# A decoder layer in fp32: state updates as row tiles, fp32r transposes, a column-tiled gate product, and another order of units

## The chip, the cores and the metric

The program runs on one core of a Trainium2 chip. The metric is the time of one execution on the device in microseconds, the median of several runs. Everything works in fp32: weights and activations come from memory as fp32, and the large products run on TensorE in a form called fp32r, of which three products make up one fp32 product.

## The reference

One layer handles a prompt of 256 tokens and 8 samples of 8 new tokens each, 320 columns in all, which share every weight. `c` conditions the layer through `w_ada`; the sample tokens start from a stored attention state and stored pooling rows.

```python
mod = jax.nn.silu(c) @ w_ada + b_ada
sh1, sc1, g1, sh2, sc2, g2 = split(mod, 6)                 # each 2048 wide
h = rmsnorm(x, norm1_g) * (1 + sc1) + sh1
q, k, v, og, u, ga, gb, alr = split(h @ w_in)              # 1024 1024 2048 2048 1024 2048 2048 16
loga = log_sigmoid(alr @ w_a2 + b_a) / 16
# per head (4 heads, 256 x 512), in chunks:  S = diag(exp(b_last)) S + kd^T v;  o = qe S + (causal qe ke^T) v
o, s_new = _gla(q, k, v, loga, s0)
y_a = rmsnorm(o, gla_norm_g) * silu(og)
d = (mean of the last 2, 4, 8 or 16 rows of u, by head) - u
y_b = (d @ w_pool[head]) * pool_scale
x = x + g1 * ((sigmoid(ga) * y_a + sigmoid(gb) * y_b) @ w_o)
h2 = rmsnorm(x, norm2_g) * (1 + sc2) + sh2
x = x + g2 * ((silu(gate) * up) @ w_down)                  # gate, up = split(h2 @ w_gu), 5632 each
y = rmsnorm(x, final_norm_g)
```

The outputs are y for the prompt and the samples, the new attention state of both and the new pooling rows of both.

## The kernel before

Activations stand transposed: 128 channels on the partitions, 320 tokens along the row, 16 such tiles for 2048 channels. Each fp32 matrix is used as a sum of two fp32r parts, hi and lo. ScalarE (ACT) casts a weight chunk to its hi part (L157), VectorE (DVE) subtracts to get the lo part (L158), and `mm3` makes three products (L171 to L173: hi by hi, hi by the activation's lo part, lo by hi).

`proj` takes one unit of 256 output columns: 16 channel tiles, two halves, three products, so 96 products of 320 columns with weights of 128 x 128 into one PSUM tile. Raw weights come on the SyncE queue. Such a unit's PSUM tile comes from the pool `pmain`, which has two; all small products take one-bank tiles from `pmisc`, which has four, through `misc()`.

**Stages.** In the head stage the rows of x are normed, the first sections of the modulation are made, and the units of attention head 0 are computed in six slices of the channels (`SLICES`); in its last slice stands `alr_proj`, the gate rank product. Then come heads 1 to 3, eleven units each, in the order q, k, v, v, u, og, og, ga, ga, gb, gb. After that w_o with x1 (8 units), the second norm, the FFN in two parts (44 units of gate and up, 8 units of w_down, each part), and the final norm with transposes of x into rows (L1107 and the lines around it).

**What sets the order.** Attention and pooling of a head are lists of steps (`gla_steps`, `pool_steps`). They stand in a queue, and `pump` takes up to ten of them after each unit. So the steps of head 0 lie between the units of head 1, and those of head 1 partly between those of head 2. The steps of a head join the queue after its unit u. `s_y`, the pooling product with w_pool (PSUM tiles `psy`, taken from `pmain`), stands for head 0 in the middle of the steps, after the attention's exponentials:

```python
    queue += pst + st[:PSY] + [sig0] + psy + st[PSY:] + [merge_step(g0, E)]
    RATE = 10
    BURST_UNITS = (None, (1, 3, 9, 10)) + ((0, 1, 2, 3, 6, 8, 9, 10),) * 2
    LOAD_UNITS = (None, (0, 1, 7, 9, 10)) + ((0, 1, 2, 5, 6, 8, 9, 10),) * 2
```

The rest of the modulation is made in bursts of column-tiled fp32 products (`ada_burst`, L301), placed by `BURST_UNITS`; their weights `araw` are loaded on the GpSimd (POOL) queue (L269) at the places in `LOAD_UNITS`. Within this, a scheduler that simulates the engines moves instructions among each other, unless `high_priority` or `issue_after` binds them.

**The steps that matter here.** All are per head. `s_att` makes the causal products within 32-row blocks as column tiles (L682, 32 records), and the cross products (L687). `s_nat2` and `s_kpn` transpose v and k of the samples with `tr` (L135, an fp32 product with the identity). `s_kpn` copies each sample's 32 rows of k into its own quarter of a zeroed tile `kpn` (named w in the order), so that a product over all 128 rows updates one sample's state. `s_state` does two such updates: a product into a `misc()` tile (L807), then state times decay plus product on DVE (L809). `s_load` loads four samples' states `S`, two tiles of 1 MB at a time (two buffers), and the store `o_gs` empties them. `s_inter` (L782, L786) multiplies queries by the states as column tiles. `s_gk` multiplies `alr`, the gate rank rows, by `w_a2` (L591).

The last lines compute the norm of y: squares summed in `acc2` by DVE, three products with ones, then Sqrt and reciprocal for each of three row blocks, and six scalings (L1121 on ACT), each with its store.

Of the kernel before, what the change touches and what calls it, by code (L numbers as in the profile page):

```python
# [11 lines left out]
F32 = mybir.dt.float32  # L12
# [8 lines left out]
P = 128  # L21
# [3 lines left out]
D = 2048  # L25
# [54 lines left out]
def body(tc, A):  # L80
# [55 lines left out]


    more = []
    last_raw = []
    last_mm = []  # L140
# [11 lines left out]
    def split(raw):  # L152
# [5 lines left out]
        V.tensor_sub(lo, raw, hi.bitcast(F32))  # L158
        return hi, lo
# [15 lines left out]
    def proj(w, col, k0, k1, xh, xl, between=None):  # L175

        ps = pmain.tile([P, 2, 512], F32, tag="pm", name=nm("ps"))
        for c0 in range(k0, k1, 4):
            nk = min(4, k1 - c0)
            for j, whi, wlo in split_chunk(w[:, c0:c0 + nk, col:col + 256], nk, 256):  # L180
                kt = c0 + j
                for i in range(2):
                    mm3(ps[:, i, :T], whi[:, i * P:(i + 1) * P], wlo[:, i * P:(i + 1) * P],
                        xh[kt], xl[kt], kt == k0, kt == k1 - 1)
            if between:
                between(c0 - k0)
# [167 lines left out]
    def new_group(h):  # L354
# [5 lines left out]
        g.u = gp.tile([P, 2, UEW], F32, tag="u", name=nm("u"))  # L360
        return g

    def new_gates(g):
        g.og = gp.tile([P, 4, T], F32, tag="og", name=nm("og"))
        g.ga = merged[2] if g.h == 0 else None
        g.gb = merged[g.h]
# [36 lines left out]
    def gates(g, kind, i, src):  # L403
        og, gb = g.og[:, 2 * i:2 * i + 2, :], g.gb[:, 2 * i:2 * i + 2, :]
        if kind == "gb":
            S.activation(gb, src, AF.Sigmoid)
            return
        sg = gp.tile([P, 2, T], F32, tag="sg", name=nm("sg"))
# [12 lines left out]


    with tc.tile_pool(name="head", bufs=1) as xp:
# [8 lines left out]
        make_identity(nc, ident)  # L432
        pt = misc()
# [57 lines left out]
        def alr_proj(walr, cum):  # L491
            V.tensor_copy(cumr, cum)
            pa = misc()
            for k0 in range(0, KT, 8):
                wal = []
                for tag in ("whi", "wlo"):
                    t = wp.tile([P, 8, 64], F32R, tag=tag, bufs=WB, name=nm("wal"))
                    G.memset(t.bitcast(F32), 0.0)
                    wal.append(t)
                wk = walr[:, k0:k0 + 8]  # L500
                S.copy(wal[0][:, :, 0:16], wk)
                V.tensor_sub(wal[1][:, :, 0:16], wk, wal[0][:, :, 0:16].bitcast(F32))
# [4 lines left out]
            G.memset(alr[32:33, :], 1.0)  # L507
            V.tensor_copy(alr[0:16, 0:T], pa[0:16, 0:T])
# [637 lines left out]
```

## Time and profile before

| | |
|---|---|
| three runs | 1977.17, 1979.94, 1980.54 us |
| median | 1979.94 us |
| the profiled execution | 1972.99 us |
| its span (first to last instruction) | 1971.2 us |
| mean granted TensorE clock | 0.993 |
| memory read, written | 373.90 MB, 24.67 MB |

The profile comes from one execution. Its rows read as follows. A group of instructions has its line, engine and operation, then out<-in by the program's names, the shape (partitions x elements), its count, busy time and the mean ns of one, and at the end the idle time of that engine just before them with what ended it. PE is TensorE's matmul, PEld its weight load, which overlaps PE. Matmul records overlap each other too: one of 320 columns lasts about 310 ns, while the next starts sooner, so what a product costs is read from start to start. The chain that ended last lists, in order of time, the work that each step waited for, with start and length. The stages view gives, for each stretch, its length, the busy time and count of PE, PEld, DVE, ACT and POOL, the granted clock (1.00 is full speed), the busy share of the DMA engines and GB/s.

### The profile page before, as it was taken

To read this page: it belongs to the slowest core of one execution; us is meant where nothing else is said; L and a number is where in the kernel's file an instruction comes from. 1 tells how busy PE (TensorE), PEld (TensorE's weight loads), DVE (VectorE), ACT (ScalarE), POOL (GpSimd) and SP (SyncE) were. 2 spreads that over 40 slices of the span, in tenths; PEclk is the share of its full clock that TensorE was granted. 3 is DMA by queue.
4 is the path that set the end of the run, shared out by engine and by line. 5 is a ranking of instruction groups with operands and counts; after the bars stand their busy time and mean duration, and the time that the engine had idled before them with its cause. 6 is when DMAs were issued, how large, how long until landed. Compare 5 with 4: busy or idle time off the path is not lost.

```text
span 1971.2 us, 34613 instructions
## 1 busy us (share of the span) xinstructions
PE 1924.5 (98%) x13808; PEld 1825.2 (93%) x13808; DVE 1007.0 (51%) x1935; ACT 826.9 (42%) x1485; POOL 207.3 (11%) x323
## 2 busy tenths in 40 slices
PE   5999999999999999999999999999999999999997
PEld 4889888988998899989989999999999999999997
DVE  3776454666355535665574444444444444444554
ACT  4433343544345433553354333333333434344443
POOL 2231131221121112111030000000000000000000
PEclk9999989999999999999999999999999999999998
DMA  9996647777875788579845555444545444444442
GB/s 349 354 354 237 203 150 264 219 230 251 256 223 188 247 268 272 183 249 321 269 153 158 186 188 182 145 150 144 156 145 155 150 150 150 150 151 144 149 139 98
DMA packets 287308, 400.60 MB, mean 203 GB/s; under 512 B 11953, under 2 KB 243921, under 8 KB 286809
## 3 DMA queue, kind: packets, MB, share of 16 engines
q1 hardware_dynamic: 250170, 261.81, 42.7%
q0 software_dynamic: 36976, 136.57, 19.5%
q8 instruction: 108, 1.77, 0.4%
q14 instruction: 54, 0.44, 0.1%
HBM read 373.90 MB, written 24.67 MB: 202 GB/s over the span
## 4 chain that ended last, share of the span: by engine, by line
PE 82%; DMA 3%; ACT 1%; DVE 0%; issue 0%; POOL 0%; ACTq 0%; DVEq 0%
PE ps L172 25%; PE ps L171 25%; PE ps L173 25%; PE pm L301 3%; PE pm L135 1%; DMA araw<-w_ada 1%; PE pm L786 1%; PE pm L807 1%; DMA raw<-w_o 1%; DMA S<-state_gla 1%; PE pm L752 1%; DMA o_gs<-S 0%; PE pm L782 0%; PE pm L591 0%; PE pm L741 0%; PE psy L171 0%
## 5 line engine op out<-in xcount | busy, mean ns | idle before, releaser
L158 DVE TENSOR_TENSOR wlo<-raw,whi 128x512 fp32r<-128x512 f32 x952 | 657.7, 694 | 792.4 <-ACT whi L157 779.9
L157 ACT CAST whi<-raw 128x512 fp32r<-128x512 f32 x952 | 587.8, 622 | 948.3 <-PE ps L172 830.1
L171 PE MATMUL ps<-hh,whi 128*128 128x320 f32 x1408 | 441.9, 314 | 6.1 <-ACT hh L337 2.6
L172 PE MATMUL ps<-hl,whi 128*128 128x320 f32 x1408 | 440.4, 313 | 0.0
L173 PE MATMUL ps<-hh,wlo 128*128 128x320 f32 x1408 | 437.4, 312 | 0.0
L172 PE MATMUL ps<-h2l,whi 128*128 128x320 f32 x1408 | 434.7, 309 | 0.0
L171 PE MATMUL ps<-h2h,whi 128*128 128x320 f32 x1408 | 434.7, 309 | 0.0
L173 PE MATMUL ps<-h2h,wlo 128*128 128x320 f32 x1408 | 434.2, 309 | 0.0
L171 PEld LDWEIGHTS ps<-hh,whi 128*128 128x128 f32 x1408 | 265.2, 188 | 19.7 <-issue 9.0
L172 PEld LDWEIGHTS ps<-hl,whi 128*128 128x128 f32 x1408 | 265.3, 188 | 10.4 <-issue 9.4
L173 PEld LDWEIGHTS ps<-hh,wlo 128*128 128x128 f32 x1408 | 264.7, 188 | 8.0 <-issue 5.3
L171 PEld LDWEIGHTS ps<-h2h,whi 128*128 128x128 f32 x1408 | 264.4, 188 | 3.4 <-ACT ah L337 3.4
L172 PEld LDWEIGHTS ps<-h2l,whi 128*128 128x128 f32 x1408 | 264.5, 188 | 0.1
L173 PEld LDWEIGHTS ps<-h2h,wlo 128*128 128x128 f32 x1408 | 264.5, 188 | 0.0
L171 PE MATMUL ps<-ah,whi 128*128 128x320 f32 x704 | 217.7, 309 | 0.0
L172 PE MATMUL ps<-al,whi 128*128 128x320 f32 x704 | 216.5, 308 | 0.0
L173 PE MATMUL ps<-ah,wlo 128*128 128x320 f32 x704 | 216.5, 308 | 0.0
L172 PEld LDWEIGHTS ps<-al,whi 128*128 128x128 f32 x704 | 132.0, 187 | 0.0
L171 PEld LDWEIGHTS ps<-ah,whi 128*128 128x128 f32 x704 | 131.9, 187 | 0.0
L173 PEld LDWEIGHTS ps<-ah,wlo 128*128 128x128 f32 x704 | 131.9, 187 | 0.0
L269 POOL DMA_DIRECT2D araw<-w_ada x64 | 55.1, 864 | 397.2 <-PE pm L301 385.9
L172 PE MATMUL ps<-ml,whi 128*128 128x320 f32 x256 | 79.3, 310 | 0.0
(282 smaller groups left out, 1634.2 us busy)
## 6 DMA issues: line engine op xcount, KB each, us to landing
raw<-w_gu SPq DMA_DIRECT2D x176, 512.0 KB, 3.5
raw<-w_in SPq DMA_DIRECT2D x170, 512.0 KB, 4.4
araw<-w_ada POOLq DMA_DIRECT2D x64, 1024.0 KB, 8.7
raw<-w_down SPq DMA_DIRECT2D x80, 512.0 KB, 3.5
hraw<-w_ada POOLq DMA_DIRECT2D x28, 1024.0 KB, 9.8
S<-state_gla POOLq DMA_DIRECT2D x16, 1024.0 KB, 8.3
o_gs<-S POOLq DMA_DIRECT2D x16, 1024.0 KB, 6.9
raw<-w_o SPq DMA_DIRECT2D x32, 512.0 KB, 6.2
```

The source lines that it names most:

```text
L135: PE.transpose(out, in_, ident[:k, :k])
L157: S.copy(hi, raw)
L158: V.tensor_sub(lo, raw, hi.bitcast(F32))
L171: PE.matmul(ps, lhsT=whi, rhs=xhi, start=start, stop=False)
L172: PE.matmul(ps, lhsT=whi, rhs=xlo, start=False, stop=False)
L173: last_mm[:] = [PE.matmul(ps, lhsT=wlo, rhs=xhi, start=False, stop=stop).ins]
L269: nc.gpsimd.dma_start(t[:, r:r + step], wada[:, k0 + r:k0 + r + step, col:col + nb * P])
L301: PE.matmul(ps[32 * j:32 * j + 32, 0:w], lhsT=scT[:, k0 + r + j, :], rhs=ada_raw[n][:, r + j, :], start=k0 == 0 and first, stop=k0 + nk == ...
L752: PE.matmul(pt, lhsT=E["kdn"][:, s, d * P:(d + 1) * P], rhs=E["vn"][:, s], start=s == 0, stop=s == 1)
L786: PE.matmul(pt[32 * j:32 * j + 32, :], lhsT=qeP[:, d, 4 * gg + j, :], rhs=E["S0", gg, d][:, j], start=False, stop=d == 0, tile_position=(0 ...
L807: PE.matmul(pt, lhsT=E["kpn"][:, j, d * P:(d + 1) * P], rhs=E["vp"][:, gg], start=True, stop=True)
```

## The change

- **State updates.** `kpn` is one tile without zeroes, written by one copy. `s_state` handles four samples at once: four `misc()` tiles, a one-element memset on DVE for each, then four products of 32 rows as row tiles (`tile_position` (32 j, 0)), bound to follow each other, and four DVE updates.
- **Transposes.** `s_nat2` and `s_kpn` use `trr`, which transposes in fp32r.
- **Gate rank.** `alr_proj` makes fp32 products with 32-column tiles, four at a time into four row groups of one tile, half of them for the hi part of h and half for the lo part. `alr` then holds four partial sums, and `w_a2` is loaded four times below each other, so that L591's product adds them.
- **Attention.** The 32 records of `s_att` are bound together at high priority, in reverse order.
- **Order.** Heads 1 and 2 take their gb units first. The attention steps of a head join the queue after its v units, not after u; the pooling steps go to the front of the queue after u. For head 0, psy stands behind all attention steps, the stored pooling rows are loaded and transposed in the head stage, and the state loads come after the exponentials, released by EX. `BURST_UNITS` and `LOAD_UNITS` are new. In w_o, the w_ada pieces are issued one per unit half: at channel chunk 8 and behind the second residual.
- **End.** In the last unit of w_down, the last four channel tiles are sorted by half; squares of that unit are summed on TensorE; one Sqrt and one reciprocal serve all row blocks.

```diff
+    def trr(out, in_):
+
+        PE.transpose(out.bitcast(F32R), in_, identr)
...
-    def proj(w, col, k0, k1, xh, xl, between=None):
+    def proj(w, col, k0, k1, xh, xl, between=None, halves=False):
...
+            if halves and c0 + nk == k1:
+                parts.sort(key=lambda p: p[0])
...
         def alr_proj(walr, cum):
...
-                for j in range(8):
-                    k = k0 + j
-                    mm3(pa[:64, 0:T], wal[0][:, j], wal[1][:, j], hh[k], hl[k], k == 0, k == KT - 1)
+            with tc.high_priority(), tc.issue_after(last_mm[0]):
+                for r in range(0, KT, 4):
+                    for n, x in enumerate((hh, hl)):
+                        for j in range(4):
+                            PE.matmul(pa[32 * j:32 * j + 32, 0:T], lhsT=walr[:, r + j, :], rhs=x[r + j].bitcast(F32),
+                                      start=r + n == 0, stop=r == KT - 4 and n == 1, tile_position=(0, 32 * j))
...
-            nc.gpsimd.dma_start(wa2[0:16, :], A["w_a2"][0, :, DK * h:DK * h + DK])
-            nc.gpsimd.dma_start(wa2[32:33, :], A["b_a"][:, DK * h:DK * h + DK])
+            for j in range(4):
+                nc.gpsimd.dma_start(wa2[32 * j:32 * j + 16, :], A["w_a2"][0, :, DK * h:DK * h + DK])
+            nc.gpsimd.dma_start(wa2[16:17, :], A["b_a"][:, DK * h:DK * h + DK])
...
+                        with tc.high_priority(), tc.issue_after(first) if first else nullcontext():
+                            mm = PE.matmul(pa[32 * j:32 * j + 32, ko:ko + P],
+                                           lhsT=E["EK"][:, d, n * P + 32 * j:n * P + 32 * j + 32], rhs=rhs,
+                                           start=d == 1, stop=d == 0, tile_position=(0, 32 * j))
+                        first = first or mm.ins
...
-                kpn = E["kpn"] = w4([P, 4, DK], F32R)
-                G.memset(kpn.bitcast(F32), 0.0)
+                kpn = E["kpn"] = w4([P, DK], F32R)
...
-                for j in range(4):
-                    sl = slice(32 * j, 32 * j + 32)
-                    if j % 2:
-                        V.tensor_copy(kpn[sl, j, :], pt[sl, 0:DK])
-                    else:
-                        S.copy(kpn[sl, j, :], pt[sl, 0:DK])
+                S.copy(kpn, pt[:, 0:DK])
...
-                    if gg == 0 and d == 0 and h > 0:
-                        after = anchor(g.v[:, 2, 0:1])
+                    if gg == 0 and d == 0:
+                        after = anchor(g.v[:, 2, 0:1] if h > 0 else E["EX"][:, 1, 0:1])
...
-                for j in (j0, j0 + 1):
-                    pt = misc()
-                    PE.matmul(pt, lhsT=E["kpn"][:, j, d * P:(d + 1) * P], rhs=E["vp"][:, gg], start=True, stop=True)
+                pts = [misc() for j in range(4)]
+                for j in range(4):
+                    V.memset(pts[j][0:1, 0:1], 0.0)
+                last = None
+                for j in (3, 2, 1, 0):
+                    sl = slice(32 * j, 32 * j + 32)
+                    with tc.high_priority(), tc.issue_after(last) if last else nullcontext():
+                        mm = PE.matmul(pts[j], lhsT=E["kpn"][sl, d * P:(d + 1) * P], rhs=E["vp"][sl, gg], start=True,
+                                       stop=True, tile_position=(32 * j, 0))
+                    last = mm.ins
...
-        st += [s_load(0), s_load(1), s_wa2, s_gk, s_exp(0), s_exp(1), s_prod, s_vstack, s_nat2, s_nat3, s_attP,
+        st += [s_wa2, s_gk, s_exp(0), s_exp(1), s_load(0), s_load(1), s_prod, s_vstack, s_nat2, s_nat3, s_attP,
...
-    queue += pst + st[:PSY] + [sig0] + psy + st[PSY:] + [merge_step(g0, E)]
+    queue += pst + st[:PSY] + [sig0] + st[PSY:] + psy + [merge_step(g0, E)]
...
+    BURST_UNITS = (None, (1, 3, 9, 10), (0, 2, 3, 4, 5, 7, 9, 10), (1, 2, 3, 4, 6, 7, 9, 10))
+    LOAD_UNITS = (None, (0, 1, 7, 9, 10)) + BURST_UNITS[2:]
...
+        order = units(h) if h == 3 else units(h)[9:] + units(h)[:9]
...
+            if kind == "v" and i == 1:
+                pump(len(queue))
+                queue += st
             if kind == "u":
-                pump(len(queue))
-                st, E = gla_steps(g)
                 pst, psy = pool_steps(g)
-                queue += pst + st
+                queue[:0] = pst
...
+            if kind == "v" and i == 0:
+                pump(len(queue))
+                queue += [st.pop(0) for _ in range(4)]
+                pump(len(queue))
...
+        if c == 8 and ui > 0 and ada_want:
+            go = fp.tile([P, 1], F32, tag="go", bufs=2, name=nm("go"))
+            V.tensor_copy(go, last_hi[0][:, 0, 0:1].bitcast(F32))
+            ada_piece(anchor(go))
...
-            if ada_want:
+            if ada_want and i == 1:
...
-                    sq_acc(acc2, k, k == 0)
+                    if ui < 7:
+                        sq_acc(acc2[:, 0:T], k, k == 0)
+                    else:
+                        S.activation(sqs[i][:, 0:T], x1[k], AF.Square)
...
+    with tc.high_priority():
+        S.activation(rr, pss[:, 0:6], AF.Sqrt, scale=1.0 / D, bias=epst)
+        V.reciprocal(rr, rr)
```

Three places on TensorE show how this moves instructions. In the rows below, hh and hl are the parts of h, whi and wlo those of a weight chunk, and x3 means three such rows running.

The first place is the pooling product of head 0 (psy, whose rows have dh, the pooled rows). Before, it stands straight behind the last unit of the head stage, `ps_2821`:

```order
L171 MATMUL ps_2821<-hh_101,whi_2942 128x320
L172 MATMUL ps_2821<-hl_117,whi_2942 128x320
L173 MATMUL ps_2821<-hh_101,wlo_2943 128x320
L171 MATMUL psy_3051<-dh_2746,whi_3055 128x320
L172 MATMUL psy_3051<-dl_2747,whi_3055 128x320
L173 MATMUL psy_3051<-dh_2746,wlo_3056 128x320
```

After the change (its products are L179 to L181) it stands some 200 rows later, behind a unit of head 1, `ps_3374`, and a group of the state updates of head 0 (L902) stands between its two PSUM tiles, `psy_3530` and `psy_3531`:

```order
L181 MATMUL ps_3374<-hh_102,wlo_3484 128x320
L179 MATMUL psy_3530<-dh_2724,whi_3534 128x320
L180 MATMUL psy_3530<-dl_2725,whi_3534 128x320
L181 MATMUL psy_3530<-dh_2724,wlo_3535 128x320
...
L181 MATMUL psy_3530<-dh_2724,wlo_3551 128x320
L902 MATMUL pm_3053<-vp_2982,w_491_3010 128x512
L902 MATMUL pm_3052<-vp_2982,w_491_3010 128x512
L902 MATMUL pm_3051<-vp_2982,w_491_3010 128x512
L902 MATMUL pm_3050<-vp_2982,w_491_3010 128x512
L179 MATMUL psy_3531<-dh_2724,whi_3534 128x320
```

So psy moved from the border of two stages into the units of head 1, and the rows show one group of four updates as it stands in the new kernel.

The second place is where such updates stood before, also for head 0: three together (L807) and then single ones between main products.

```order
L171 MATMUL ps_3749<-hh_86,whi_3752 128x320
L135 MATMUL pm_3527<-cst,osn_3525 128x128 x4
L807 MATMUL pm_3536<-vp_3000,w_578_3506 128x512
L807 MATMUL pm_3539<-vp_3000,w_578_3506 128x512
L807 MATMUL pm_3542<-vp_3000,w_578_3506 128x512
L172 MATMUL ps_3749<-hl_102,whi_3752 128x320
...
L172 MATMUL ps_3749<-hl_106,whi_3786 128x320
L807 MATMUL pm_3545<-vp_3000,w_578_3506 128x512
L173 MATMUL ps_3749<-hh_90,wlo_3787 128x320
```

The products of a head that stood alone or in twos and threes now stand in fours, each four with its own row tiles.

The third place is the block products of `s_att` for head 0. Before, they come in three visits (sixteen records, then eight and eight; an fp32 product makes two records a row), with transposes and main products between:

```order
L682 MATMUL pm_3302<-w_545_3303,EQK_2780 32x128 x3
L682 MATMUL pm_3302<-EQK_2780 32x128
...
L687 MATMUL pm_3325<-w_487_2978,EX_2782 128x128 x2
L135 MATMUL pm_3332<-cst,v_202 128x128 x4
L173 MATMUL ps_3588<-hh_90,wlo_3626 128x320
...
L682 MATMUL pm_3302<-w_546_3306,EQK_2780 32x128 x3
L682 MATMUL pm_3302<-EQK_2780 32x128
L173 MATMUL ps_3588<-hh_91,wlo_3626 128x320
L682 MATMUL pm_3302<-w_546_3306,EQK_2780 32x128 x3
```

After the change all of them (L778) stand together:

```order
L179 MATMUL ps_3578<-hh_101,whi_3687 128x320
L778 MATMUL pm_3084<-w_510_3088,EQK_2753 32x128 x3
L778 MATMUL pm_3084<-EQK_2753 32x128
...
L778 MATMUL pm_3084<-w_509_3085,EQK_2753 32x128 x3
L778 MATMUL pm_3084<-EQK_2753 32x128
L784 MATMUL pm_3107<-w_457_2814,EX_2755 128x128
```

The three visits became one, with the cross products (L784) behind it.

More of the change, by code (lines that the diff above doesn't have):

```diff
@@ L432, in body @@
         make_identity(nc, ident)
+        S.copy(identr, ident)
         pt = misc()
@@ L549, in body @@
                     alr_proj(walr, cum)
+                if last and ui == 0:
+                    pst, psy = pool_steps(g0)
+                    pst.pop(0)()
+                    pst.pop(0)()
                 if last and ui in (0, 1):
@@ L675, in s_att @@
                 qj.append(t)
-            for n in range(2):
+            first = None
+            for n in (1, 0):
                 ko = 0 if n == 0 else 2 * P
-                for d in range(2):
+                for d in (1, 0):
                     for j in range(4):
```

253 lines of the change are left out of this document (125 added, 128 removed).

## Prediction

> **What bounds the kernel now.** I read the page first, then busy time by stage, then the chain of work that ended last, and last the timeline of the few places where TensorE waits.
>
> ```profile
> span 1971.2 us, 34613 instructions
> PE 1924.5 (98%) x13808; PEld 1825.2 (93%) x13808; DVE 1007.0 (51%) x1935; ACT 826.9 (42%) x1485; POOL 207.3 (11%) x323
> PE 82%; DMA 3%; ACT 1%; DVE 0%; issue 0%; POOL 0%; ACTq 0%; DVEq 0%
> 1300.00:1600.00 300.00, 300.00 (x2048) 300.00 (x2047) 136.66 (x231) 113.11 (x182) 0.00 (x0) 1.00 0.48 150
> ```
>
> TensorE (PE) is busy nearly all the time and carries the chain; no other engine comes near. In the undisturbed stage (the stages view: stretch, PE busy and count, the other engines, granted clock, DMA share) 2048 main products of 320 columns take 300 us: **0.1465 us for each**, loads hidden. The change leaves all 11,328 main products alone. So it can gain in three ways: less TensorE time in the small products, fewer waits of TensorE, a shorter end. I price each against the profiled run.
>
> **State updates (L807, then L902).**
>
> ```profile
> L807 PE MATMUL pm<-vp,w 128*128 128x512 f32 x64 | 23.2, 403 | 0.0
> 296.67 0.86 PE pm L782 x2
> 297.52 1.85 PE pm L786 x16
> 299.38 0.34 PE ps L172
> 310.66 0.71 PE pm L807 x3
> 404.32 0.87 PE pm L135 x8
> ```
>
> The rows under the first are of the chain (start, length), where lengths are true steps. Three updates take 0.71, so 0.237 each, and 64 take 15.2 us. Now four updates stand together as row tiles, each with a weight load of its own, 16 groups in all. No row tile ran in the trace. The nearest row is L786, four column tiles at a time: 16 records in 1.85, where one record of the same 512 columns takes 0.43 alone (0.86 for two). Four rounds of 0.43 are 1.72, so the tiles do run side by side, and 0.13 is left for getting into the tiled mode. The main product behind it takes 0.34 where 0.1465 is usual: 0.19 for getting out. A group then costs 0.19 (in, with full weights of 128 columns, as on the way out) + 0.237 + 3 x 0.007 (1.85 less 1.72 leaves no more between tiles) + 0.19 = 0.64, and 16 cost 10.3 us: **4.8 saved**. Bounds: no switching cost, 15.2 - 16 x 0.26 = 11.0 saved; tiles that run one after another, 4 x 0.237 + 0.38 = 1.33 a group, 6.1 lost. I take the value by L786, the nearest row.
>
> The Trainium skill, "TensorEngine Tiling (Array Packing)", section "Key Properties", says that changing the tiling mode drains the engine. This speaks against many small tiled groups; the trace agrees, with 0.13 in and 0.19 out. Without the drain the updates would save 11.0 rather than 4.8. The skill's "TensorE: Matmul & The Clock Gate", Part 3, gives four row tiles of this size 3.07 times the speed of single ones; by it, as an estimate, a group takes 0.05 more and the sum of all parts would be 17.6 instead of 18.4.
>
> **Attention tiles (L682, then L778).**
>
> ```profile
> 430.14 0.57 PE pm L682 x16
> 432.67 0.36 PE pm L682 x8
> 433.03 0.34 PE ps L172
> ```
>
> For each head the 32 records came in three visits (16, 8, 8), with full products between. Eight records more cost 0.57 - 0.36 = 0.21, so a visit has 0.15 of its own, and 0.19 on the product behind it. One visit instead of three saves 2 x 0.34, in four heads 2.7: I take **2.6**, between 0 (were L778 broken up again) and 2.7.
>
> **The gate rank product (L491, then L593).**
>
> ```profile
> L173 PE MATMUL pm<-hh,wal 128*64 128x320 f32 x16 | 4.9, 308 | 0.0
> 198.05 0.31 PE L171 MATMUL pm<-hh,wal 128*64 128x320 f32 x1
> 198.20 0.31 PE L172 MATMUL pm<-hl,wal 128*64 128x320 f32 x1
> ```
>
> 48 products (16 on each of three lines) start 0.147 apart: 7.0 us. Now 32 fp32 products, two records each, run four at a time: 16 rounds. A round of 512 columns is 0.43 (L786), so 320 columns cost 0.27; 16 x 0.27 + 0.32 for in and out = 4.6. **2.4 saved**, 0 to 2.6.
>
> **Transposes of v and k in fp32r (L141).** Eight take 0.87, 0.109 each.
>
> ```profile
> 285.90 0.41 PEld L618 LDWEIGHTS pm<-cumr,w 128*128 128x128 f32 x3
> ```
>
> Three weight loads of 128 columns for fp32r, 0.19 long each, span 0.41: they start 0.11 apart. A transpose needs one such load, and one pass over 128 columns would be shorter than that, so the load sets the same 0.109. I take **0**; were loads hidden, 48 x 0.055 = 2.6.
>
> **The pooling product of head 0 (psy).** This is the largest term.
>
> ```profile
> 261.73 0.31 PE L173 MATMUL ps<-hh,wlo 128*128 128x320 f32 x1
> 264.46 0.63 PE L171 MATMUL psy<-dh,whi 128*128 128x320 f32 x1 [2.42 <-ACT dh L337]
> ...
> 265.75 0.47 PE L173 MATMUL psy<-dh,wlo 128*128 128x320 f32 x1
> ...
> 269.72 0.64 PE L171 MATMUL psy<-dh,whi 128*128 128x320 f32 x1 [1.10 <-DVE mg L914]
> ...
> 272.82 0.47 PE L173 MATMUL psy<-dh,wlo 128*128 128x320 f32 x1
> 262.00:266.00 4.00, 1.35 (x4) 0.97 (x4) 2.42 (x9) 1.27 (x2) 1.83 (x4) 0.76 1.07 336
> 266.00:270.00 4.00, 2.90 (x11) 2.50 (x11) 1.01 (x2) 0.00 (x0) 2.37 (x6) 0.50 0.44 127
> 270.00:274.00 4.00, 4.00 (x15) 3.82 (x16) 1.36 (x3) 1.24 (x2) 0.00 (x0) 0.50 0.00 0
> 274.00:278.00 4.00, 4.00 (x26) 3.84 (x25) 0.94 (x2) 3.13 (x5) 0.00 (x0) 0.96 0.46 130
> ```
>
> TensorE waited for the pooled rows dh, then for a free PSUM tile, and with the wait the granted clock fell to 0.50 for some 10 us. From 262.04 (261.73 + 0.31) to 273.29 (272.82 + 0.47) 24 products took 11.25 us; at 0.1465 they need 3.5. That is 7.7 lost. In the new order the pooled rows' inputs (L135 on w) stand some 230 main products, 34 us, ahead of psy; twelve products on the first PSUM tile and a state group stand ahead of the second. Both waits lose their cause. I take **7.6 saved**; 3 if the second wait and part of the clock loss stay.
>
> The skill's "TensorE: Matmul & The Clock Gate", Part 1, has the full clock back after about 3.4 us of sustained work. The trace differs: 0.50 from 266 to 274. By the page the loss, and so the gain, would be some 3.4 smaller, and the sum 15.0.
>
> **Smaller terms.**
>
> ```profile
> PE pm L786 <- DMA S<-state_gla: 0.6, 1, 0.6
> PE pm L301 <- DMA araw<-w_ada: 1.0, 2, 0.5
> S<-state_gla POOLq DMA_DIRECT2D x16, 1024.0 KB, 8.3
> 288.45 0.34 ACT EQK L623 x2
> 318.73 0.76 DVE S L809
> ```
>
> - The one wait for a state load (0.6) goes: the second pair of loads of head 0 now has about 34 us from the first group to its reader, against a store and a load in a row. **0.6 saved.**
> - Head 0's first loads are now anchored on EX (a copy on POOL that waits for ACT; the loads and the next w_ada pieces queue behind it). EX comes about 2 us after the gate sums (exponentials end near 288.8). From those sums to the reader L875 stand 77 main products and small ones, 14.5 us; 2.5 + 0.8 of issue + 8.3 to landing leave 3 us. Cost **0**; without that cover, see the second rival.
> - Each w_a2 load becomes four, three more issues on POOL for each head: POOL is 11% busy and the loads stand well ahead of the gate product. **0.**
> - Bursts of w_ada products (L301) wait for their loads where two stand close. Bursts 82 main products apart or less are seven in the old order, of which two waited 0.5; there are nine in the new. **0.3 lost**, 0 to 4. Spreading the last pieces over w_o takes no wait that TensorE shows: 0.
> - 64 one-element memsets, and the table loads that go, are on DVE and ACT at 51% and 42%: 0.
>
> **The end.**
>
> ```profile
> 1954.91 0.48 DVE x L991
> 1957.18 1.72 PE pm L135 x6
> 1958.90 0.97 PE pm L1107 x6
> 1960.44 1.09 ACT yn L1121
> ```
>
> The halved last unit should bring nothing: both halves share one PSUM tile, and in the new order, as in the old, only the first residual waits for TensorE and the second does not, so the first waits for the last product. What goes are the two adds, the norm products behind the transposes (0.97), and two of three square roots. But both transposes and the last copies to yn still stand ahead of ACT's scaling at 1960.44, so of about 2.2 only **0.7** comes through; 0 to 2.2.
>
> **The sum.** 4.8 + 2.6 + 2.4 + 7.6 + 0.6 - 0.3 + 0.7 = 18.4 us. The profiled execution took 1972.99 (span 1971.2 and 1.8 around it); it would take 1954.6. It lies 6.95 below the median of the runs shown, 1979.94, and I take the saving from the median: **1961.5**.
>
> **Rivals.**
>
> - **Row tiles don't overlap.** For it: no row tile has run here. Against it: column tiles do, and loads into different rows need not meet. 6.1 lost instead of 4.8 saved is 10.9 worse: 1972.4.
> - **A new long wait halves the clock.** One wait of 2.4 cost 7.7. Candidates are head 0's first state loads (3 us of slack, beside main weights) or one state group. For it: two 1 MB loads are issued together. Against it: waits of 0.5 and 0.6 elsewhere left the clock alone. Once: 1969.2.
> - **fp32r transposes run at one pass**, loads hidden: 2.6 more, 1958.9. Against it is the load row.
> - **State groups wait for banks, and the kernel is slower.** A group needs all four pmisc banks at once, and its four DVE memsets wait for them, TensorE behind. DVE empties a bank in 0.76 (row above), four in 3 us, while groups of a pair stand 45 main products, 6.6 us, apart; so it should fit. But if other tenants (burst, transposes) hold a bank, every group waits. The point is 18.4 / 16 = 1.15 us a group; at 2 us a group it is 32 lost, 13.6 over before: 1993.
>
> **How the numbers follow.** Forecast 0.66 (1955 to 1968, as bursts, end and psy take their bounds), no overlap 0.10, one long wait 0.11, faster transposes 0.06, bank waits 0.04, and 0.03 that several small losses leave nothing. The range 1952 to 1974 takes in the first four but for their tails. 0.2% of the median, 4 us, is about what a measurement of this kernel tells from no change: faster 0.91, same 0.04, slower 0.05.
>
> **What would show it.** Right: L902 groups near 0.26 with a long product behind each; L778 in one visit a head; granted clock 1.00 at psy of head 0 and no wait there; psy products 0.147 apart. Wrong: L902 records 0.237 apart; a stretch of clock 0.50 after the first 40 us and before the end; TensorE waiting for memsets or for S; L141 below 0.1. The sum fails most easily if TensorE's freed time returns as waits on w_ada.

## The result, and the profile after

The changed kernel takes 1958.91 us (median of 4 executions, 1958.44 to 1961.26), the kernel before 1978.74 (4, 1977.17 to 1980.54): a ratio of 0.9902, 95% interval 0.9885 to 0.9919. A second comparison on another occasion gave 1958.82 against 1974.48, a ratio of 0.9916 (0.9902 to 0.9930). The forecast was 1961.5.

The two profiled executions lie closer together than the medians: 1972.99 before, 1961.26 after, 11.7 us. The prediction put the second of them at 1954.6. So its sum, 18.4, has to be checked term by term, not by its total. The stages view of both kernels (stretch, length, busy time and count of PE, PEld, DVE, ACT and POOL, granted clock, DMA share, GB/s), cut at the first product of the head stage, the first and the last of w_o, the first of w_down's first part, and the last of all; before first, then after:

```profile
32.30:883.50 851.20, 841.25 (x6332) 760.93 (x6333) 480.84 (x991) 374.41 (x711) 163.75 (x241) 0.99 0.75 247
883.50:1002.00 118.50, 117.64 (x842) 114.94 (x844) 62.75 (x131) 46.73 (x86) 14.14 (x24) 1.00 0.84 276
1002.00:1330.50 328.50, 327.84 (x2258) 315.19 (x2258) 157.58 (x261) 138.14 (x242) 19.86 (x38) 1.00 0.53 167
1330.50:1954.90 624.40, 624.37 (x4268) 624.01 (x4266) 291.45 (x504) 247.85 (x416) 0.23 (x2) 1.00 0.47 144
1954.90:1971.20 16.30, 2.67 (x12) 2.26 (x12) 5.69 (x18) 5.99 (x12) 0.00 (x0) 0.57 0.47 161
```

```profile
32.70:870.80 838.10, 830.34 (x6383) 746.28 (x6384) 477.63 (x1040) 361.85 (x697) 160.16 (x241) 1.00 0.76 254
870.80:990.10 119.30, 116.50 (x807) 113.74 (x810) 63.03 (x135) 46.85 (x85) 15.60 (x26) 1.00 0.75 251
990.10:1318.70 328.60, 327.94 (x2259) 315.24 (x2259) 157.46 (x261) 138.34 (x242) 19.98 (x39) 1.00 0.52 167
1318.70:1943.00 624.30, 624.30 (x4271) 624.21 (x4269) 291.53 (x504) 247.71 (x416) 0.41 (x4) 1.00 0.46 144
1943.00:1959.50 16.50, 4.60 (x25) 4.12 (x24) 4.55 (x14) 5.86 (x10) 0.00 (x0) 0.56 0.47 159
```

The reader is to see that the gain of 13.1 us is in the attention stages, and that w_o, in the second rows, is 0.8 us longer although it holds 35 TensorE instructions less (a burst of w_ada products, with its transposes, moved out of it). The FFN is the same, and the end too.

The small products came out as priced. The chain that ended last in the changed kernel, at one state group, one attention visit, one visit of transposes, and the gate rank product (start, length):

```profile
196.59 4.44 PE pm L593 x64
279.14 0.63 PE pm L141 x8
307.36 0.15 PE ps L180
307.51 0.44 PE pm L902 x4
307.94 0.34 PE ps L181
308.29 0.15 PE ps L179
314.60 1.01 PE pm L778 x32
```

Four row tiles take 0.44 together, where one update alone took 0.237, and the product behind them 0.34: 0.44 + 0.19 = 0.63 a group, the forecast 0.64. The attention's 32 records take 1.01 in one visit, against 0.57 + 0.36 + 0.36 in three. The gate rank product takes 4.44, the forecast 4.6 with the way out.

Two losses are new. The waits view of TensorE for the changed kernel (what waited for what: us in total, times, longest) has them in its first two rows here; the fourth is the row of the kernel before that answers to the first:

```profile
PE ps L179 <- ACT whi L164: 3.6, 4, 1.2
PE ps L179 <- DVE mg L511: 2.6, 1, 2.6
PE pm L311 <- DMA araw<-w_ada: 0.9, 1, 0.9
PE ps L171 <- ACT whi L157: 0.7, 1, 0.7
```

The second stands at 662.6 us, where a unit of head 3 needs a PSUM tile that still holds psy of head 2. The timeline there (start, length, instruction, idle before and what ended it), and the stages view behind the wait:

```profile
656.21 1.28 ACT L106 ACT_TABLE_LOAD   x1
657.50 0.53 ACT L110 ACTIVATE acc<-pm,epst 128x320 f32<-128x320 f32 x1
658.05 1.28 ACT L419 ACT_TABLE_LOAD   x1
659.34 0.70 ACT L419 ACTIVATE sg<-ps 128x640 f32<-128x640 f32 x1
660.06 1.28 ACT L111 ACT_TABLE_LOAD   x1
661.36 0.47 ACT L111 ACTIVATE acc<-acc 128x320 f32<-128x320 f32 x1
661.86 1.94 DVE L927 SCALAR_TENSOR_TENSOR EQK<-EQK,vec,acc 128x320 f32<-128x320 f32 x4 [4.91 <-ACT acc L111]
663.72 0.48 DVE L942 TENSOR_TENSOR EQK<-EQK,og 128x320 f32<-128x320 f32 x1
664.12 1.00 DVE L511 SCALAR_TENSOR_TENSOR mg<-psy,vec,mg 128x320 f32<-128x320 f32 x2
665.18 0.63 PE L179 MATMUL ps<-hh,whi 128*128 128x320 f32 x1 [2.60 <-DVE mg L511]
```

```profile
665.00:668.50 3.50, 3.32 (x12) 3.33 (x13) 3.50 (x10) 0.00 (x0) 0.00 (x0) 0.51 1.02 358
```

DVE works in order: the emptying of psy (L511) stands behind the norm's scaling (L927), which had DVE idle for 4.91 us until ACT had the inverse square root. ACT makes it as Ln (L110) and Exp (L111). Here the sigmoid of a gate unit (L419) stands between the two, so ACT loads its function tables three times, 1.28 us each; the kernel before has no table load at that Exp. TensorE waits 2.6 us, and then the clock is at half.

### The profile page after: what moved, and what is told of

It reads as the page before. It is cut to its first block, busy times and chain, and to the rows that moved or that the text cites. A ratio compares the mean times of both kernels' runs of the same rounds, so it can differ in the third digit from the quotient of the medians.

```text
span 1959.5 us, 34717 instructions
## 1 busy us (share of the span) xinstructions
PE 1915.1 (98%) x13838; PEld 1811.5 (92%) x13838; DVE 1003.4 (51%) x1985; ACT 815.9 (42%) x1470; POOL 206.1 (11%) x329
## 3 DMA queue, kind: packets, MB, share of 16 engines
q8 instruction: 108, 1.77, 0.4%
## 4 chain that ended last, share of the span: by engine, by line
PE 93%; DMA 2%; DVE 1%; SPq 1%; ACT 1%; issue 0%; ACTq 0%; POOL 0%; DVEq 0%
PE ps L179 28%; PE ps L180 28%; PE ps L181 28%; PE pm L311 3%; PE pm L135 1%; PE pm L246 1%; DMA raw<-w_o 1%; DMA raw<-w_in 1%; PE pm L875 1%; PE pm L841 1%; SPq L235 1%; DVE wlo L165 1%; DMA araw<-w_ada 1%; PE pm L871 0%; PE pm L902 0%
## 5 line engine op out<-in xcount | busy, mean ns | idle before, releaser
L179 PE MATMUL ps<-hh,whi 128*128 128x320 f32 x1408 | 442.3, 315 | 9.2 <-DVE mg L511 2.6
L181 PE MATMUL ps<-hh,wlo 128*128 128x320 f32 x1408 | 438.1, 312 | 0.0
L179 PE MATMUL ps<-h2h,whi 128*128 128x320 f32 x1408 | 434.7, 309 | 0.0
L181 PE MATMUL ps<-h2h,wlo 128*128 128x320 f32 x1408 | 434.2, 309 | 0.0
L179 PEld LDWEIGHTS ps<-hh,whi 128*128 128x128 f32 x1408 | 265.7, 189 | 23.8 <-issue 10.3
L181 PEld LDWEIGHTS ps<-hh,wlo 128*128 128x128 f32 x1408 | 265.3, 189 | 7.6 <-issue 6.5
L179 PEld LDWEIGHTS ps<-h2h,whi 128*128 128x128 f32 x1408 | 264.4, 188 | 3.4 <-ACT ah L347 3.4
L181 PEld LDWEIGHTS ps<-h2h,wlo 128*128 128x128 f32 x1408 | 264.5, 188 | 0.0
L179 PE MATMUL ps<-ah,whi 128*128 128x320 f32 x704 | 218.2, 310 | 0.0
L181 PE MATMUL ps<-ah,wlo 128*128 128x320 f32 x704 | 217.0, 308 | 0.0
L179 PEld LDWEIGHTS ps<-ah,whi 128*128 128x128 f32 x704 | 132.2, 188 | 0.0
L181 PEld LDWEIGHTS ps<-ah,wlo 128*128 128x128 f32 x704 | 132.2, 188 | 0.0
L179 PE MATMUL ps<-mh,whi 128*128 128x320 f32 x256 | 79.4, 310 | 2.3 <-ACT whi L164 2.3
```

Of the source, the lines that this page charges most:

```text
L179: PE.matmul(ps, lhsT=whi, rhs=xhi, start=start, stop=False)
L181: last_mm[:] = [PE.matmul(ps, lhsT=wlo, rhs=xhi, start=False, stop=stop).ins]
```

## The experiments

Each kernel was run for a profile and timed against the kernel before. The changed kernel itself was timed on two of the four occasions (1958.91 and 1958.82), while the median of the kernel before moved between 1974.48 and 1978.74 over all four; so a difference of 2 or 3 us from the changed kernel on another occasion shows little by itself. Sums over products below run from the end of one product to the end of the next.

**Both kernels again.** No edit.

> The kernel before, unchanged. The profiled pair differs by 11.7 us (1972.99 to 1961.26), the medians by 19.8 us. Theory A: the profiled execution of before was a lucky one and a typical one is 4 to 6 us longer in some place that the change removes or moves; then this profile (1976 to 1980) shows more waits of TensorE or a longer time at clock 0.50, and the place can be named. Theory B: the difference of execution to execution is spread over all stages, or lies in the head of the program that the change leaves alone; then no single stage is over 2 us longer than in the first profile. Ratio to itself 1.000 within 0.002.

The kernel before: 1975.31 (11 executions, 1971.17 to 1979.61), ratio to itself 0.9999 (0.9986 to 1.0011); its profile took 1975.08. Cut at the same products, its stages are 852.1, 119.1, 328.6, 624.3 and 16.25 us, against 851.3, 118.4, 328.6, 624.3 and 16.35: no stage is over 1 us longer, theory B, though at 1975.08 this was not one of the slow executions either. Over all 56 executions of it on four occasions the times go from 1970.98 to 1985.75, with a median of 1975.4.

> The changed kernel, unchanged, for a second profile and as the base of the other runs. Theory A: the wait of 2.6 us for the psy evacuation of head 2 near 662 us and the 3.4 us at clock 0.50 behind it, and the waits of some 4 us on w_o weights, stand in every execution; then they show again within 0.5 us, at 1958 to 1962 us. Theory B: they belong to the one execution that was profiled; then they are gone here and the time is 1954 to 1957 us.

1958.82 (4, 1957.46 to 1959.68), profile 1959.68. The wait for L511 is 2.60 again and the clock halved behind it; the w_o products take 115.96 instead of 117.11. Theory A.

**The w_ada pieces in w_o.** The pieces go back behind every residual:

```diff
-        if c == 8 and ui > 0 and ada_want:
...
-            ada_piece(anchor(go))
...
-            if ada_want and i == 1:
+            if ada_want:
```

> The changed kernel with the last w_ada pieces in w_o issued as before (one behind every residual). Theory A: the pieces at channel chunk 8 make TensorE wait for w_o weights, and 768 products of w_o cost 117.1 us instead of 113.0; undone, the w_o products fall back to 113 to 114 us and the time falls by 2 to 4 us against the changed kernel. Theory B: the w_o weights come late because units of 16 us with 2 MB of weights and 2 MB of w_ada pieces need the memory anyhow; then the waits move to other units or to the bursts and the time stays within 1 us.

The 768 products of w_o take 113.2 instead of 117.1 and 116.0, and the stage of w_o (stages view) no longer has PE idle:

```profile
869.30:984.80 115.50, 115.50 (x807) 113.82 (x810) 63.11 (x132) 46.90 (x85) 12.08 (x22) 1.00 0.79 259
```

PE is busy for all 115.50 us, where the changed kernel had 116.50 of 119.30. In the changed kernel's chain stands what it waited for, two loads of w_o weights that took over 10 us, and POOL's timeline has two pieces issued within 1 us of each; here those at the first:

```profile
923.76 10.20 DMA raw<-w_o
939.66 10.27 DMA raw<-w_o
```

```profile
923.13 0.79 POOL L279 DMA_DIRECT2D araw<-w_ada  x1
924.40 0.75 POOL L279 DMA_DIRECT2D araw<-w_ada  x1
```

So theory A holds for the stage: the place of the pieces makes the waits. How it does is argued only. Loads of w_o weights as long stand in the kernel before (12.1 us) and in this one (11.4), and there TensorE waits for none of them; so it is not the length alone, but which weights are late. For the time, theory A's 2 to 4 us are not shown: the profiled execution took 1954.62, but the median, 1957.90 (4), is only 0.9 below the changed kernel's, less than the scatter of either.

**The norm behind the evacuation.** For heads 0 to 2, L927's scaling moves into the merge, behind psy's last evacuation:

```diff
-            for e in range(4):
+            E["rs"] = rs
+            for e in range(4 if h == H - 1 else 0):
                 V.scalar_tensor_tensor(o[:, e], o[:, e], GNG[:, e:e + 1], rs, op0=ALU.mult, op1=ALU.mult)
...
+            for e in range(4 if g.h < H - 1 else 0):
+                o = E["o"][:, e]
+                with tc.issue_after(last_evac[0]):
+                    V.scalar_tensor_tensor(o, o, GNG[:, e:e + 1], E["rs"], op0=ALU.mult, op1=ALU.mult)
```

> The changed kernel with one edit: for heads 0 to 2 the norm's scaling of o on DVE stands behind the evacuation of the psy tiles instead of ahead of it. Theory A: TensorE's wait near 662 us comes from psy evacuations queued on DVE behind that scaling, which waits for ACT; with the edit the wait of 2.6 us and the time at clock 0.50 behind it (1.6 us more) go: 4 us less than the changed kernel. Theory B: the PSUM tile comes late for another reason (ACT's table loads, weights); then the wait stays within 1 us and so does the time.

The same place in the stages view of this kernel:

```profile
662.00:665.00 3.00, 2.98 (x21) 2.72 (x20) 1.38 (x4) 2.11 (x5) 2.45 (x3) 1.00 0.56 164
665.00:668.50 3.50, 3.50 (x26) 3.50 (x25) 3.50 (x9) 1.24 (x2) 0.00 (x0) 1.00 0.97 343
```

PE is busy throughout, with 26 products in the second stretch where the changed kernel had 12 (at a clock of 0.51). The stretch from the first product to w_o takes 834.4 us, against 838.0 and 839.2: theory A, 3.6 to 4.8 us. The median is 1956.71 (4, 1955.19 to 1959.01). ACT's three table loads are still there; only what stands behind them on DVE has changed. All seven profiles with the wait of 2.60 near 662 have the sigmoid between Ln and Exp at that place. In those with single state updates and with plain transposes (below) Ln and Exp stand next to each other there, and that wait is gone. A kernel in which the two were bound together was not run.

**Both edits at once** (the two diffs above).

> The changed kernel with both edits at once: the norm's scaling behind the psy evacuation (heads 0 to 2), and the w_ada pieces in w_o issued as before. Theory A (two separate losses): the wait near 662 us and the time at clock 0.50 behind it are gone, the w_o products cost 113 to 114 us instead of 116 to 117; the profiled execution takes 1951 to 1954 us and the median lies 4 to 6 us under that of the changed kernel (1958.8). Theory B (one freed wait returns as another): one of the two sums stays high, and the median stays within 2 us of 1956.7, that of the first edit alone.

1954.53 (4, 1953.53 to 1955.08), ratio to before 0.9891 (0.9871 to 0.9910). All four lie below all eight executions of the changed kernel (1957.46 and up), though on another occasion, and the intervals of the two ratios overlap. w_o takes 115.1 us and the wait at 662 is gone; the two losses are separate. Its profile shows a burst that waited 2.0 us for its w_ada load near 494 us, with the clock halved there, so not all of the 4 us shows each time.

**psy of head 0 at its old place.**

```diff
-    queue += pst + st[:PSY] + [sig0] + st[PSY:] + psy + [merge_step(g0, E)]
+    queue += pst + st[:PSY] + [sig0] + psy + st[PSY:] + [merge_step(g0, E)]
```

> The changed kernel with the pooling product of head 0 (psy) at its old place, behind the first twelve attention steps, the rest as changed. Theory A (the place made the waits): TensorE waits again for the pooled rows and for a PSUM tile, the clock is 0.50 for 7 to 10 us, and the 96 psy products of all heads cost 22 to 23 us instead of 14.9; the time is 6 to 8 us over the changed kernel's. Theory B (the stored rows loaded early and the freer queue already make dh come in time): psy stays at 15 to 17 us and the time within 2 us.

Theory A fell. psy stands at 259.70 us, straight behind a unit as before, and does not wait; all psy products cost 14.9 us (the changed kernel 15.1, before 23.0). The median is 1960.76 (6, 1957.82 to 1963.23). The move that the prediction credited with 7.6 us isn't what saved it.

**And the stored pooling rows at their old place.** The two steps that load and transpose them go back to the start of the queue:

```diff
                     pst, psy = pool_steps(g0)
-                    pst.pop(0)()
-                    pst.pop(0)()
```

With psy moved back too:

> The changed kernel with psy of head 0 at its old place, and with the load and transposes of head 0's stored pooling rows at their old place too (the start of the queue, behind the head stage). With psy alone moved back the 96 psy products stayed at 14.7 us without a wait, against my working. Theory A (the stored rows came late, and with them dh): with both back, TensorE waits 2 to 3 us for dh, the clock falls to 0.50 for 7 to 10 us, psy costs 21 to 23 us, and the time is 5 to 8 us over that of psy alone moved back (1960.8). Theory B (something else in the new order, such as the free POOL queue or the state loads behind EX, lets dh come in time): psy stays at 15 to 16 us.

1960.76 (6, 1957.54 to 1963.94), and psy costs 14.9 us: the wait doesn't come back (timeline, and the clock in the stages view):

```profile
250.47 0.37 PE L135 MATMUL pm<-cst,sp 120*128 120x120 f32 x2
261.77 0.31 PE L179 MATMUL psy<-dh,whi 128*128 128x320 f32 x1
```

```profile
266.00:270.00 4.00, 4.00 (x30) 4.00 (x29) 2.70 (x5) 3.99 (x6) 0.00 (x0) 1.00 0.02 7
```

Theory B again. What differs is the load of the stored rows (tile sp): the steps are back, but not the load. POOL's timeline, this kernel first, then before:

```profile
3.11 0.69 POOL L445 DMA_DIRECT2D sp<-state_pool  x1
```

```profile
250.87 0.53 POOL L569 MEMSET qeP<- 128x512 f32 x1 [9.26 <-PE pm L135]
...
252.41 0.59 POOL L848 DMA_DIRECT2D sp<-state_pool  x1
...
253.43 0.71 POOL L866 COPY w<-u 128x64 f32<-128x64 f32 x1
254.23 1.53 POOL L775 DMA_DIRECT2D S<-state_gla  x2
```

Before, the load was issued at 252.41, behind memsets that had waited for the end of the head stage: sp came from the pool `lp`, which takes over the head stage's memory. It landed 3.0 us later; its transposes stand at 258.81, the window sums after them, and dh at 263.68. The diff takes sp from `gp`, which is there from the start:

```diff
-            E["sp"] = lp.tile([NB * PB, 256], F32, tag="sp", name=nm("sp"))
+            E["sp"] = gp.tile([NB * PB, 256], F32, tag="sp", name=nm("sp"))
```

The scheduler then issues the load at 3.11 us. With it, the transposes run at 250.47, 8 us earlier. That one word, `lp` to `gp`, is the likely cause by these rows; a kernel with it alone put back was not run. A rival is left: the state loads behind EX were in this run too. Before, they were issued at 254.23, behind the load of sp, which took 3.0 us to land against 2.5 in this kernel; that explains little of the 8 us, unless the scheduler placed the transposes by it.

This edit alone, with psy at its new place:

> The changed kernel with only the load and transposes of head 0's stored pooling rows put back to the start of the queue; psy stays at its new place behind the attention steps. Theory A (either of the two moves is enough, since at the new place dh has 34 us): psy stays at 14.9 us, the time within 2 us of the changed kernel (1958.8). Theory B (the late rows delay other steps of the queue, since POOL and DVE run in order): waits of 1 us or more appear between 258 and 330 us and the time is 2 us or more longer.

psy stays at 14.7 us. The time is 1961.97 (6, 1959.57 to 1963.00): 3 us over the changed kernel. But none of the waits between 258 and 330 us that theory B expected is there: the longest new ones are 1.5 us for an evacuation of v (L405) at 133.5, in the head stage, and 0.85 for one of psy (L511) at 462.9. Here too the load is issued at 3.11 us, so only the transposes are later (251.2 instead of 201.0), and neither edit shows what late rows would cost. So both places are to spare for psy; where the 3 us come from is not settled.

**State updates one by one.** The zeroed tile and 64 products of 128 rows come back:

```diff
-                pts = [misc() for j in range(4)]
...
+                for j in range(4):
+                    pt = misc()
+                    PE.matmul(pt, lhsT=E["kpn"][:, j, d * P:(d + 1) * P], rhs=E["vp"][:, gg], start=True, stop=True)
```

> The changed kernel with the state updates as before: a zeroed tile of four quarters and 64 single products of 128 rows in place of 16 groups of four row tiles. Theory A (the working of the prediction): 64 at 0.235 make 15.0 us where the groups cost 16 x (0.434 + 0.200) = 10.1; the attention stages get 4 to 5 us longer and so does the time. Theory B (the bank waits of four tiles at once, or the memsets, take the gain back elsewhere): the stages get less than 2 us longer or shorter.

1965.29 (6, 1962.77 to 1968.19), 6 us over the changed kernel. The 64 products cost 15.5 us; the row tiles 6.95 and 16 x 0.20 behind them, 10.15: 5.3 of TensorE time, as theory A has it. The stage from the first product to w_o takes 843.9 us instead of 838.0 and 839.2, though the wait near 662 is gone in this order and the clock stays at 1.00 behind it; other places lost what that saved. So the 5.3 are shown, but the 6 us of the total are not these alone.

**Plain transposes.**

```diff
-        PE.transpose(out.bitcast(F32R), in_, identr)
+        PE.transpose(out, in_.bitcast(F32), ident)
```

> The changed kernel with the transposes of v and k (48 of them) as fp32 products with the identity, as before. The prediction put fp32r at nothing saved, the trace of the changed kernel shows 0.63 for eight and 0.07 more on the product behind them, against 0.87. Theory A (one pass, loads partly hidden): undone, they cost 0.109 each again, 0.17 more for each visit of eight and 0.02 for each visit of two: 0.9 us in all, which the stage sums show and the median hardly. Theory B (what was freed was waiting anyway): the stage from the first main product to w_o stays as long within 0.3 us.

The chain's row for a visit of eight, here and (shown above) 0.63 in fp32r:

```profile
281.22 0.87 PE pm L141 x8
```

The 48 transposes cost 5.24 us against 3.53, less about 0.07 behind each of twelve visits: 0.9 us, as theory A has it. The total can't tell it: 1961.43 (6, 1959.42 to 1964.77), and 841.8 us to w_o, in an order in which the wait for L511 was gone and bursts waited 2.8 us for their loads instead of 0.9.

**The old end.** No halves, three norms and three square roots as before:

```diff
-            ps = proj(wdn, 256 * ui, f0, f1, ah, al, halves=pi == 1 and ui == 7)
+            ps = proj(wdn, 256 * ui, f0, f1, ah, al)
...
-                    if ui < 7:
-                        sq_acc(acc2[:, 0:T], k, k == 0)
-                    else:
+                    sq_acc(acc2[:, 0:T], k, k == 0)
...
-        S.activation(rr, pss[:, 0:6], AF.Sqrt, scale=1.0 / D, bias=epst)
+        S.activation(rr[:n, 2 * a:2 * a + 2], pt[:n, 2 * a:2 * a + 2], AF.Sqrt, scale=1.0 / D, bias=epst[:n])
```

> The changed kernel with the end as before (no halves, squares summed on DVE, three square roots and reciprocals). The prediction put the new end at 0.7 saved, 0 to 2.2. From the last product of w_down to the end of the span the profiles of before show 16.35 and 16.25 us, those with the new end 16.5, 15.2, 15.2, 15.3, 15.3, 16.6, 15.8 and 15.5. Theory A: the old end gives 16.2 to 16.4 again, 0.7 over the mean of the new. Theory B: the difference is in the scatter of the clock at the end: it gives 15.2 to 15.8.

From the last product to the end of the span: 15.74 us. The eleven profiles with the new end give 15.2 to 16.8, mean 15.7; the two of before 16.25 and 16.35. Neither theory is ruled out; by these three profiles of the old end the new one gains 0 to 0.6 us on average, less than the new end's own scatter. The median, 1961.39 (5), doesn't help: in its profile the w_o stage took 122.3 us.

**The old order of units.** Heads 1 and 2 take gb last:

```diff
-        order = units(h) if h == 3 else units(h)[9:] + units(h)[:9]
+        order = units(h)
```

> The changed kernel with heads 1 and 2 taking their units in the old order, gb last, and the bursts at the same unit numbers. The prediction put the order of units at nothing. Theory A (gb first pushes the norm of head 2 against its psy evacuation): with gb last the norm's scaling stands well ahead of the evacuation, the wait of some 3 us near 662 us is gone, and the time is 2 to 4 us less than 1958.8. Theory B (gb last moves other waits in: bursts, evacuations): the wait goes but main products and bursts together cost as much, and the time stays within 2 us.

Neither theory: 1968.90 (10, 1962.63 to 1972.26), 10 us slower than the changed kernel. The wait at 662 is gone, but worse ones stand in head 0's steps. The timeline at its psy, and the stages view behind:

```profile
302.25 2.72 DVE L907 SCALAR_TENSOR_TENSOR S<-S,dec,pm 128x512 f32<-128x512 f32 x4
304.89 0.55 DVE L511 SCALAR_TENSOR_TENSOR mg<-psy,vec,mg 128x320 f32<-128x320 f32 x1
305.36 0.54 DVE L511 SCALAR_TENSOR_TENSOR mg<-psy,vec,mg 128x320 f32<-128x320 f32 x1
305.95 0.63 PE L179 MATMUL psy<-dh,whi 128*128 128x320 f32 x1 [2.46 <-DVE pm L897]
```

```profile
308.00:312.00 4.00, 2.55 (x11) 1.83 (x7) 3.59 (x7) 0.93 (x2) 1.31 (x2) 0.50 0.40 155
```

A state group stands in the middle of psy's first tile here. Its four updates take DVE 2.72 us, the tile's evacuation (L511) and the memsets of the next group (L897) come behind them, and TensorE waits 2.46 us for the second tile, then goes at half clock for 10 us. In the changed kernel's timeline the evacuation is ahead of the updates:

```profile
299.14 1.01 DVE L511 SCALAR_TENSOR_TENSOR mg<-psy,vec,mg 128x320 f32<-128x320 f32 x2 [0.26 <-PE psy L181]
300.06 1.40 DVE L907 SCALAR_TENSOR_TENSOR S<-S,dec,pm 128x512 f32<-128x512 f32 x2
```

So what decides at this place is where an evacuation stands on DVE, as at 662 us. Two more waits stand beside it: 2.19 us at 280.3, for a copy of q on ACT (L407), and 1.58 at 312.1, for an attention tile from DVE (L767). The rival "state groups wait for banks" of the prediction had the engine and the four updates (3 us), though not this victim.

## Why the prediction held, step by step

| term | forecast | shown |
|---|---|---|
| state groups | -4.8 | -4.6 (14.76 to 10.15) |
| attention in one visit | -2.6 | -2.7 (four heads, 0.67 each) |
| gate rank | -2.4 | -2.5 (7.03 to 4.57) |
| fp32r transposes | 0 | -0.9 |
| psy of head 0 | -7.6 | -7.9 (23.0 to 15.1), by another cause |
| wait for S | -0.6 | gone |
| bursts' waits | +0.3 | 1.0 before, 0.9 after |
| w_ada pieces in w_o | 0 | +4.1 (113.0 to 117.1), +2.7 in the second profiles |
| norm ahead of psy's evacuation | a rival, 0.11 | +3.6 to +4.8 |
| the end | -0.7 | +0.1 in this pair, -0.6 over the profiles, 0.0 against the old end alone |

The shown terms add up to about -11, close to the -11.7 between the two profiled executions. The median over all executions, 1975.4 before and 1958.8 after, differs by 16.6. So the forecast of 18.4 was right in direction and near in size, but in part by luck, because two things offset: losses of some 7 to 8 us that the sum had at nothing, and typical executions of before that are slower than the one profiled. Where these executions lose their time is open; no stage of the second profile stands out.

Right in mechanism and size: the state groups, attention, and gate rank. The groups and the gate rank were priced by column tiles, the attention by its own three visits; of the three, only the groups were undone in a run. The rival of row tiles that don't overlap is out, by 0.44 for four.

**psy.** "Both waits lose their cause" through the new place: the sum was right, the step was wrong. With psy at its old place the waits are gone as well; the rows that dh needs came 8 us earlier, so the right sum was luck. I had traced the wait to dh, and not further back to the load at 252.41.

**fp32r transposes.** I took the spacing of weight loads, 0.11, as the floor. Eight in 0.63 are 0.079 apart, so it isn't one for this form; 0.07 behind each visit takes part of the gain back.

**w_o.** "Takes no wait that TensorE shows: 0". The row I had priced by was that of the waits before; I counted how many pieces run in a unit, not beside which weights each would be issued.

**The new long wait.** The rival was named and priced by one wait (7.7), but with the wrong candidates. It came from ACT's table loads, with a sigmoid between Ln and Exp, through DVE's order, and cost 3.6 to 4.8.

**The order of units** had no price at all. Undone, it costs 10 us (8.5 to 9.7 of it in the stage up to w_o), by a rival close to the one that was given 0.04.

## What to carry to other kernels

When a wait goes, follow its chain back to the first instruction that was late, and test that one: here it was not the place of the product that made the 8 us, but, as far as the rows show, a load's memory pool. A load into a tile whose pool takes over used memory stood behind the end of the head stage, at 252.41 us; from a pool that was open from the start it went out at 3.11. On a saturated engine, small savings priced from neighbouring rows add up well; the error lies in queues that run in order (DVE behind ACT, POOL loads beside weights), so look at what stands ahead of each evacuation after a reorder, and on ACT at what has come between two functions of one table.

## What the runs showed of the hardware

The granted clock goes in steps of 3.413 us: all records at 0.50 inside the kernels last 3.41, 6.83 or 10.24 us. The same wait of 2.60 us near 662 us halved the clock in five profiles and left it at 1.00 in two (that with the old w_o pieces and that with the old end). The steps' borders, counted on from the clock's records, tell them apart. Where 1.9 to 2.6 us of the wait fell into one step, the next step ran at half; where it was split into 1.57 and 1.03 or into 1.55 and 1.05, none did. The stages view of the kernel with the old w_o pieces, behind such a wait:

```profile
666.00:669.50 3.50, 3.50 (x26) 3.50 (x25) 3.50 (x10) 0.77 (x2) 0.00 (x0) 1.00 1.03 351
```

The clock came back after the first step with next to no wait in it (0.16 us in the changed kernel). In the kernel before it stayed low for 10.24 us: the rest of the first wait (0.35) and one of 0.23 fell into the first of three steps, and a second long wait, of 1.10 us, into the second; in its second profile, where the steps lay otherwise, it stayed for 6.83. So my reading that the trace differs from the Trainium skill ("TensorE: Matmul & The Clock Gate", Part 1) was too quick: the page's free-running window of some 3.4 us, with full clock after one busy window, agrees with all of these. Where it differs is the way down: the page asks for a whole idle window, and at this place 1.9 us of 3.41 were enough, 1.57 were not. Other waits of these traces leave the border open: with the old order of units, 1.45 and 0.17 us in one step near 959 us halved the clock, and in the second profile of before 1.77 us near 477 us did not.
